# High DVE priority for the state updates, and the low-rank up-projections as two full products before two half-row ones

## Chip, cores and metric

The kernel runs on one core of a Trainium2 chip. The metric is the device time of one execution in microseconds. Engines are named as in the profile: PE is TensorE's matmuls, PEld its weight loads, DVE is VectorE, ACT ScalarE, POOL GpSimd, SP the queue that issues most transfers.

## What is computed

Two layers over 1024 tokens of width 1024. Each layer normalises its input, projects it, runs four mixers with 8 heads of 64, gates every mixer's output, and projects back:

```python
for l in range(DEPTH):                       # 2
    h = rms_norm(x, norm_pre[l])
    p = h @ w_in[l]
    (a_qk, a_v, a_o, a_z, a_i, a_f, b_sh, b_z, c_x, c_z, d_q, d_k, d_v, d_z) = split_at(...)
    h_a = mlstm_chunkwise(...)               # A: C = sc * C + (w v) k, out = C q
    b_sh = b_sh + rwkv_mu[l] * (token_shift(b_sh) - b_sh)
    r_b, k_b, v_b, w_lo, a_lo = split_at(b_sh, [G, G, G, LORA_W, LORA_A])
    decay_logit = rwkv_w0[l] + jnp.tanh(w_lo) @ rwkv_w_up[l]
    w_b = jnp.exp(-W_DECAY_SCALE * jax.nn.sigmoid(decay_logit))
    a_b = jax.nn.sigmoid(rwkv_a0[l] + a_lo @ rwkv_a_up[l])
    wkv = rwkv7_scan(...)                    # B: S = S (diag(w) - kh (a kh)) + v k, y = S r
    y_c = rglru(causal_dwconv(c_x, ...), ...) * silu(c_z)    # C
    o_d = retention_chunkwise(q_d, k_d, heads(d_v))          # D: R = g * R + k v
    y = jnp.concatenate([y_a, y_b, y_c, y_d], -1) @ w_out[l]
    x = x + rms_norm(y, norm_post[l])
```

`jnp.tanh(w_lo) @ rwkv_w_up` and `a_lo @ rwkv_a_up` are the two low-rank up-projections (64 inner columns each).

## The kernel before

**Units.** Every mixer works on four units of 128 channels (two heads): A0 to A3, B0 to B3, C0 to C3, D0 to D3. A unit has projection pieces (`ch_piece_of`, `tok_piece_of`: 24 matmuls of 512 columns for half of the tokens, or the like of 256, into the PSUM ring `pj`) and a mix; those of A, B and D go through the tokens in quarters of 256. In a layer a first stretch loads and normalises, a long middle runs projections and mixes together, and `out_product` multiplies the stored outputs by the output weights.

**Precision.** A float32 operand is split into two parts, `hi` and `lo`, of a faster type (`fp32r`), and a product is made of three matmuls. For the up-projections, `lu[0]` (tile `luh`) holds the high part of the weights twice, over 128 rows, and meets the token operand `lo_` (tile `lora`), whose 128 rows are high and low part; `lu[1]` (tile `lul`) is the low part of the weights, which meets the high part alone, so it takes 64 rows: the upper half for the decay (n = 0, result `wps`), the lower half for the other (n = 1, result `aps`). `prep` does this once for each quarter of each B unit, 4 x 4 x 2 = 32 times, and writes the head sums with `onesr` behind it.

**Unit B.** `prep` builds decays and scores; `invert` does a triangular inversion of 32 x 32 blocks on DVE, step by step (tiles `NT`, `inv`, `PA`); `mix` joins the blocks, makes `TQ` = [Q'|T] with four DVE subtractions from PSUM, and then walks four chunks of 64: a matmul of `TQ` with the state `bS`, and two DVE instructions (one for each head) that write the next `bS`, scaled by `wc`.

**Units A and D.** Per quarter: scores on PE and their weighting on DVE (`D`, a tile of the ring `t`), then two chunks of 128, each with a matmul that reads the state (`aS`, `dS`) and two DVE instructions that update it. The outputs are normalised (`ln_groups`, with a power on POOL) and, with a delay (`drv.later`), transposed on PE (`psmx<-ident,t` for A and D, `psbc<-ident,bl` for B) and stored.

**Order.** `Driver` writes the instructions in the order of a planner: the class `Clock` estimates when each engine is free, and a thread's next step is written when its `clock.step` plus a slack has passed and two PSUM banks of its ring are expected free; otherwise a projection step is written. For PE the planner adds `DRAIN` = 0.095 us when the kind of matmul changes, which is its rows, type and operation: `mode = (rows, w.dtype == F32R, name)`. The framework then lays out each engine's queue ahead of time, by its own timing: among the instructions that it expects to be ready, the one written first. `tc.high_priority()` makes the instructions written inside it count as written much earlier. On the chip each queue runs in the order so laid out. All records carry one helper's line (L255), so instructions are told apart by tiles.

Of the kernel before, what the change touches and what calls it, by code (L numbers as in the profile page):

```python
# [20 lines left out]
ALU = mybir.AluOpType  # L21
# [89 lines left out]
G128 = [float(np.exp(_log_g().astype(np.float64)[h] * 128.0)) for h in range(NH)]  # L111
# [25 lines left out]
QA = 256  # L137
QB = 256
# [123 lines left out]
def trunk(ctx: ExitStack, tc, x, wch, wa, wd, wg, wo, pv, gb, lup, lrw, npost, cst, dtab, out):  # L262
    nc = tc.nc
    clock = Clock()
    V, A, Pl, PE, DQ = (Timed(e, n, clock) for e, n in ((nc.vector, "DVE"), (nc.scalar, "ACT"), (nc.gpsimd, "POOL"), (nc.tensor, "PE"),
                                                        (nc.sync, "SP")))
# [83 lines left out]
    bS = [const.tile([128, 128], F32, tag=f"bS{i}", name=f"bS{i}") for i in range(2)]  # L350
# [422 lines left out]
    def unit_b(l, P, hTs, j, drv):  # L773
        rkvd = DT(f"rkv{l}_{j}", (3, 128, S))
        st = {"p": 0, "ready": -1, "inverted": -1}
# [32 lines left out]
        def prep(qt):  # L808
# [5 lines left out]
            lu = st["lu"]  # L814
# [6 lines left out]
            lo_ = T("lora", (128, 2, QB), F32R)  # L821
# [7 lines left out]
            wps = PT("bc")  # L829
            aps = PT("bc")  # L830
            for n, p in enumerate((wps, aps)):
                hp = slice(64 * n, 64 * n + 64)
                PE.matmul(p[:, 0:QB], lu[0][:, n, :], lo_[:, n, :], start=True, stop=False)
                PE.matmul(p[:, 0:QB], lu[1][hp], lo_[hp, n, :], start=False, stop=True)
            nps = PT("bc")
            head_sums(nps, kparts)
# [106 lines left out]
        def mix(qt):  # L943
# [62 lines left out]
            for p in range(CP):  # L1006
                for h, e in ((0, 0), (1, 1), (1, 0), (0, 1)):
                    PE.matmul(pss[e][64 * h:64 * h + 64, p * 128:(p + 1) * 128], AP[nrow(e), h * CP + p, :], Gt[nrow(e), h, 2 * p + e, 64:192], start=True, stop=True)
            for e in range(2):
                p3 = pss[e][:, 0:CP * 128].rearrange("p (c t) -> p c t", c=CP)  # L1010
                V.tensor_tensor(TQ[:, e::2, 0:64], AR[:, :, 2 + e, :], p3[:, :, 0:64], ALU.subtract)
                V.tensor_tensor(TQ[:, e::2, 64:128], id64.unsqueeze(1).to_broadcast((128, CP, 64)), p3[:, :, 64:128], ALU.subtract)
# [8 lines left out]
            for c in range(CB):  # L1021
                yc = yd[:, c * 128:(c + 1) * 128]
                n = qt * CB + c
                if n:
                    PE.matmul(yc, TQ[:, c, :], bS[n % 2], start=False, stop=True, skip_group_check=True)
                for h in range(2):
                    hp = slice(64 * h, 64 * h + 64)
                    V.tensor_scalar(bS[(n + 1) % 2][hp, hp], yc[64:128, hp], wc[64:128, h, c:c + 1], None, ALU.mult)
                if c + 1 < CB:
                    yield STEP  # L1030
            drv.flush("B")
# [57 lines left out]
    def unit_a(l, P, hTs, j, drv):  # L1089
# [28 lines left out]
        def mix():  # L1118
            yield lambda: st_["p"] == 8 and P.gates_done
            st = None  # L1120
            NQ = QA // 128
            for qt in range(S // QA):
                half, qo = divmod(qt * QA, H)
                q, k = qk[0, half][:, qo:qo + QA], qk[1, half][:, qo:qo + QA]
                c0 = qo // 128
                vq, oq = va[half][:, c0:c0 + NQ, :], tho[half][:, c0:c0 + NQ, :]
                gt = P.gT[:, 4 * half + c0:4 * half + c0 + NQ, :]
                ts_ = slice(qt * QA, (qt + 1) * QA)
                qsb = tq()
                for h in range(2):  # L1130
                    DQ.dma_start(qsb[64 * h:64 * h + 64, :], P.qdram[2 * j + h:2 * j + h + 1, ts_].to_broadcast((64, QA)))
                pk = []
                Ds = []
                for h in range(2):
                    D = tq()
                    DQ.dma_start(D, P.adram[2 * j + h:2 * j + h + 1, ts_].to_broadcast((128, QA)))
                    Ds.append(D)
                kt = tq()
                ps = PT("mx")
                for c in range(NQ):  # L1140
                    sl = slice(c * 128, c * 128 + 128)
                    PE.transpose(ps[:, sl], k[:, sl], ident)
                V.tensor_tensor(kt.rearrange("p (c h d) -> p c h d", c=NQ, h=2), ps[:, 0:QA].rearrange("p (c h d) -> p c h d", c=NQ, h=2),
                                gt[:, :, 8 + 2 * j:10 + 2 * j].unsqueeze(3).to_broadcast((128, NQ, 2, 64)), ALU.mult)
                for h in range(2):
                    D = Ds[h]
                    for c in range(NQ):
                        sl = slice(c * 128, c * 128 + 128)
                        V.scalar_tensor_tensor(D[:, sl], D[:, sl], gt[:, c, 2 * j + h:2 * j + h + 1], cap, ALU.add, ALU.min)
                    A.activation(D, D, AF.Exp)  # L1150
                yield STEP
                pss = [PT("mx"), PT("mx")]
                for c in range(NQ):
                    sl = slice(c * 128, c * 128 + 128)
                    for h in range(2):
                        hp = slice(64 * h, 64 * h + 64)
                        PE.matmul(pss[h][:, sl], k[hp, sl], q[hp, sl], start=True, stop=True)
                for h in range(2):
                    D = Ds[h]
                    V.scalar_tensor_tensor(D, pss[h][:, 0:QA], 1.0 / 32, D, ALU.mult, ALU.mult)  # L1160
                    pk.append(D)
                sc = small(NQ)
                V.tensor_copy(sc, qsb.rearrange("p (c t) -> p c t", t=128)[:, :, 127])
                q1 = qsb
                V.tensor_tensor(q1, q, qsb, ALU.mult)
                yield STEP
                xa = tq()
                dn = small(2 * NQ)
                for c in range(NQ):
                    sl = slice(c * 128, c * 128 + 128)  # L1170
                    o = PT("mx")
                    if st is not None:
                        PE.matmul(o[:, 0:130], q1[:, sl], st, start=True, stop=True)
                    for h in range(2):
                        PE.matmul(o[:, 65 * h:65 * h + 65], pk[h][:, sl], vq[:, c, 65 * h:65 * h + 65], start=(st is None and h == 0), stop=True, skip_group_check=True)
                    PE.matmul(o[:, 256:386], kt[:, sl], vq[:, c, :], start=True, stop=True)
                    o3 = o[:, 0:130].rearrange("p (h e) -> p h e", h=2)
                    V.scalar_tensor_tensor(xa[:, sl].rearrange("p (h e) -> p h e", h=2), oq[:, c, :].rearrange("p (h e) -> p h e", h=2),
                                           1.0, o3[:, :, 0:64], ALU.add, ALU.mult)
                    A.activation(dn[:, 2 * c:2 * c + 2], o3[:, :, 64], AF.Square)  # L1180
                    st2 = aS[(NQ * qt + c) % 2]
                    for h in range(2):
                        hp = slice(64 * h, 64 * h + 64)
                        if st is None:
                            V.tensor_copy(st2[hp, 65 * h:65 * h + 65], o[hp, 256 + 65 * h:256 + 65 * h + 65])
                            continue
                        V.scalar_tensor_tensor(st2[hp, 65 * h:65 * h + 65], st[hp, 65 * h:65 * h + 65], sc[hp, c:c + 1],
                                               o[hp, 256 + 65 * h:256 + 65 * h + 65], ALU.mult, ALU.add)
                    st = st2
                    yield STEP  # L1190

                V.tensor_tensor(dn.rearrange("p (c h) -> p c h", h=2), dn.rearrange("p (c h) -> p c h", h=2),
                                gt[:, :, 16 + 2 * j:18 + 2 * j], ALU.max)
                V.tensor_scalar(dn, dn, 4e-5, None, ALU.mult)
                drv.flush("A")
                yn = ln_groups(xa.rearrange("p (g d) -> p g d", d=64), 2 * NQ, dn, tq)
                if qt % 2 == 1:
                    drv.free += 4
                drv.later("A", lambda yn=yn, qt=qt: out_a(l, j, P.h_mnw, yn, qt))
                yield  # L1200
# [11 lines left out]
    def unit_d(l, P, hTs, j, drv):  # L1212
# [28 lines left out]
        def mix():  # L1241
# [3 lines left out]
            st = None  # L1245
            NQ = 2
            for qt in range(4):
# [29 lines left out]
                for c in range(2):  # L1277
# [9 lines left out]
                    for h in range(2):  # L1287
                        hp = slice(64 * h, 64 * h + 64)
                        if st is None:
                            V.tensor_copy(st2[hp, hp], o[hp, so + 64 * h:so + 64 * h + 64])  # L1290
                            continue
                        V.scalar_tensor_tensor(st2[hp, hp], st[hp, hp], G128[2 * j + h], o[hp, so + 64 * h:so + 64 * h + 64], ALU.mult, ALU.add)
                    st = st2
                    yield STEP
                ep = small(4)
# [282 lines left out]
```

## Time and profile before

| what | value |
|---|---|
| median of 3 runs | 2529.39 us (2527.3 to 2534.37) |
| profiled execution | 2524.98 us |
| its span, first to last instruction | 2523.1 us |
| PE busy | 2383.7 us, 94% |
| DVE busy | 1794.0 us, 71% |
| ACT busy | 1054.0 us, 42% |
| mean granted clock of PE | 0.992 |

The times of the rows below are microseconds from the start of the span unless marked ns. Busy time of a group is the union of its instructions; matmuls are pipelined, so one that is recorded as 0.38 us long may be followed by the next after 0.13 us. What PE spends on a matmul is read from the starts of neighbours in the timeline. The figure behind the bar of a group is the engine's idle time just before its instructions, and the arrows name what ended it.

### The profile page before, as it was taken

What the parts mean: (1) busy time and instruction counts of PE and PEld (TensorE: products, weight loads), DVE (VectorE), ACT (ScalarE), POOL (GpSimd) and SP (SyncE); (2) the same over time, 40 slices, a digit from 0 to 9 for tenths busy, and PEclk for the clock granted to TensorE, in tenths of its full rate; (3) what the DMA queues carried; (4) which work ended last, traced back from release to release, by engine and by line L of the source; (5) the groups of instructions that cost most, each with busy time, mean ns of one, the idle gap of its engine ahead of it and who ended that gap; (6) DMA issues with size and microseconds to landing.
All of it is one profiled execution on the core that took longest, in us unless ns stands there. A gap on an engine that the chain in (4) does not pass through costs nothing.

```text
span 2523.1 us, 45012 instructions
## 1 busy us (share of the span) xinstructions
PE 2383.7 (94%) x16032; PEld 1955.2 (77%) x16032; DVE 1794.0 (71%) x5724; ACT 1054.0 (42%) x2325; POOL 193.7 (8%) x306
## 2 busy tenths in 40 slices
PE   7999999999999999999999999999999999999998
PEld 5797887787787777887677878877877877788876
DVE  6678878878778875435577787888788778744464
ACT  5334433543543553323354344335445435522233
POOL 1201100010000000000012001000000000000000
PEclk9999999999999999999999999999999999999999
DMA  5323233232222233655633232332323222326564
GB/s 160 101 72 88 62 78 99 67 84 71 91 76 75 75 88 103 194 162 176 196 119 103 68 93 74 78 90 68 81 72 90 69 79 76 102 94 217 172 198 153
DMA packets 219237, 265.82 MB, mean 105 GB/s; under 512 B 72708, under 2 KB 122244, under 8 KB 219012
## 3 DMA queue, kind: packets, MB, share of 16 engines
q1 hardware_dynamic: 210308, 254.54, 33.9%
q0 software_dynamic: 8704, 8.39, 1.4%
q8 instruction: 127, 2.08, 0.3%
q14 instruction: 98, 0.80, 0.1%
HBM read 201.76 MB, written 61.08 MB: 104 GB/s over the span
## 4 chain that ended last, share of the span: by engine, by line
PE 47%; DVE 28%; DMA 10%; issue 8%; POOL 4%; ACT 2%; SPq 2%; DVEq 0%; POOLq 0%; ACTq 0%
PE pspj L255 31%; PE psbc L255 9%; PE psmx L255 7%; DVE NT L255 4%; DVE pr L255 4%; DMA PA<-pd 4%; DVE t L255 3%; DVE lo L255 2%; DVE bS L255 2%; POOL sm L255 2%; DVE bt L255 2%; DMA raw<-in_wo_dram 2%; DVE inv L255 2%; SPq L255 2%; DVE sm L255 1%
## 5 line engine op out<-in xcount | busy, mean ns | idle before, releaser
L255 PE MATMUL pspj<-hT,hi 128*128 128x512 f32 x2880 | 940.2, 405 | 2.1 <-DVE hT L255 1.4
L255 PEld LDWEIGHTS pspj<-hT,hi 128*128 128x128 f32 x2880 | 522.0, 190 | 106.7 <-issue 2.5
L255 PE MATMUL pspj<-hT,lo 128*128 128x512 f32 x1440 | 569.8, 396 | 0.0
L255 ACT CAST hi<-raw 128x512 fp32r<-128x512 f32 x372 | 230.0, 619 | 470.0 <-PE pspj L255 266.2
L255 PE MATMUL pspj<-hi,hT 128*128 128x256 f32 x2048 | 409.9, 290 | 0.0
L255 DVE TENSOR_TENSOR lo<-raw,hi 128x512 fp32r<-128x512 f32 x372 | 257.2, 693 | 152.4 <-ACT hi L255 150.9
L255 PEld LDWEIGHTS pspj<-hi,hT 128*128 128x128 f32 x2048 | 331.5, 192 | 6.7 <-issue 1.6
L255 PEld LDWEIGHTS pspj<-hT,lo 128*128 128x128 f32 x1440 | 272.5, 189 | 58.9 <-DVE lo L255 0.2
L255 PE MATMUL pspj<-lo,hT 128*128 128x256 f32 x1024 | 291.1, 284 | 0.1
L255 PEld LDWEIGHTS pspj<-lo,hT 128*128 128x128 f32 x1024 | 197.0, 192 | 0.8 <-DVE lo L255 0.5
L255 POOL TENSOR_TENSOR sm<-sm,mhalf 128x4 f32<-128x4 f32 (+1 forms) x96 | 90.8, 946 | 1227.1 <-DVE sm L255 1141.4
L255 DVE SCALAR_TENSOR_TENSOR NT<-PA,NT 128x23 f32<-128x23 f32 (+13 forms) x768 | 142.9, 235 | 49.0 <-DMA PA<-pd 45.4
L255 PE MATMUL psbc<-hi,pr 128*128 128x512 f32 x384 | 130.7, 394 | 0.0
L255 PE MATMUL pspj<-hi,pr 128*128 128x512 f32 x384 | 130.7, 394 | 0.0
L255 DVE SCALAR_TENSOR_TENSOR pr<-c,pv,pr 128x512 f32<-128x512 f32 x144 | 107.3, 745 | 15.8 <-ACT pr L255 14.9
L255 ACT ACTIVATE t<-t 128x256 f32<-128x256 f32 (+1 forms) x132 | 53.9, 411 | 150.7 <-DVE t L255 126.7
L255 PE MATMUL psmx<-pr,t 128*128 128x65 f32 (+3 forms) x768 | 108.3, 276 | 0.2 <-DVE t L255 0.2
L255 PEld LDWEIGHTS psmx<-pr,t 128*128 128x128 f32 x768 | 96.9, 192 | 1.3 <-DVE t L255 0.3
L255 PE MATMUL psmx<-hi,pr 128*128 128x512 f32 x256 | 91.2, 397 | 3.5 <-ACT pr L255 2.0
L255 DVE TENSOR_TENSOR inv<-PA,NT 128x24 f32<-128x24 f32 (+13 forms) x480 | 87.1, 181 | 8.4
L255 DVE TENSOR_TENSOR NT<-NT,inv 128x24 f32<-128x24 f32 (+13 forms) x480 | 86.6, 180 | 7.2
L255 DVE TENSOR_SCALAR bS<-psbc,wc 64x64 f32<-64x64 f32 x256 | 74.2, 290 | 17.2 <-PE psbc L255 9.8
(273 smaller groups left out, 3824.2 us busy)
## 6 DMA issues: line engine op xcount, KB each, us to landing
raw<-in_wch_dram SPq DMA_DIRECT2D x180, 256.0 KB
raw<-in_wo_dram SPq DMA_DIRECT2D x128, 256.0 KB
PA<-pd SPq DMA_DIRECT2D x64, 256.0 KB
zmix<-c SPq DMA_DIRECT2D x64, 256.0 KB
rkv<-ymix SPq DMA_DIRECT2D x64, 256.0 KB
rkv<-c SPq DMA_DIRECT2D x48, 256.0 KB
rkv<-rkv SPq DMA_DIRECT2D x32, 384.0 KB
lora<-lora POOLq DMA_DIRECT2D x32, 256.0 KB, 3.5
```

Of the source, the lines that this page charges most:

```text
L255: res = fn(*args, **kw)
```

## The change

In `prep` of unit B the four matmuls of the up-projections are written in another order: first the two 128-row products (n = 0, 1), then the two 64-row ones. Five kinds of DVE instruction are put inside `tc.high_priority()`: the four subtractions into `TQ`, the two updates of `bS`, the weighting of unit A's scores, and the updates of `aS` and `dS`. Operands, results and instruction counts stay as they are.

```diff
             for n, p in enumerate((wps, aps)):
+                PE.matmul(p[:, 0:QB], lu[0][:, n, :], lo_[:, n, :], start=True, stop=False)
+            for n, p in enumerate((wps, aps)):
                 hp = slice(64 * n, 64 * n + 64)
-                PE.matmul(p[:, 0:QB], lu[0][:, n, :], lo_[:, n, :], start=True, stop=False)
                 PE.matmul(p[:, 0:QB], lu[1][hp], lo_[hp, n, :], start=False, stop=True)
...
-            for e in range(2):
+            with tc.high_priority():
+              for e in range(2):
                 p3 = pss[e][:, 0:CP * 128].rearrange("p (c t) -> p c t", c=CP)
                 V.tensor_tensor(TQ[:, e::2, 0:64], AR[:, :, 2 + e, :], p3[:, :, 0:64], ALU.subtract)
                 V.tensor_tensor(TQ[:, e::2, 64:128], id64.unsqueeze(1).to_broadcast((128, CP, 64)), p3[:, :, 64:128], ALU.subtract)
...
-                for h in range(2):
-                    hp = slice(64 * h, 64 * h + 64)
-                    V.tensor_scalar(bS[(n + 1) % 2][hp, hp], yc[64:128, hp], wc[64:128, h, c:c + 1], None, ALU.mult)
+                with tc.high_priority():
+                    for h in range(2):
+                        hp = slice(64 * h, 64 * h + 64)
+                        V.tensor_scalar(bS[(n + 1) % 2][hp, hp], yc[64:128, hp], wc[64:128, h, c:c + 1], None, ALU.mult)
...
-                    V.scalar_tensor_tensor(D, pss[h][:, 0:QA], 1.0 / 32, D, ALU.mult, ALU.mult)
+                    with tc.high_priority():
+                        V.scalar_tensor_tensor(D, pss[h][:, 0:QA], 1.0 / 32, D, ALU.mult, ALU.mult)
...
-                        V.scalar_tensor_tensor(st2[hp, 65 * h:65 * h + 65], st[hp, 65 * h:65 * h + 65], sc[hp, c:c + 1],
-                                               o[hp, 256 + 65 * h:256 + 65 * h + 65], ALU.mult, ALU.add)
+                        with tc.high_priority():
+                            V.scalar_tensor_tensor(st2[hp, 65 * h:65 * h + 65], st[hp, 65 * h:65 * h + 65], sc[hp, c:c + 1],
+                                                   o[hp, 256 + 65 * h:256 + 65 * h + 65], ALU.mult, ALU.add)
...
-                        V.scalar_tensor_tensor(st2[hp, hp], st[hp, hp], G128[2 * j + h], o[hp, so + 64 * h:so + 64 * h + 64], ALU.mult, ALU.add)
+                        with tc.high_priority():
+                            V.scalar_tensor_tensor(st2[hp, hp], st[hp, hp], G128[2 * j + h], o[hp, so + 64 * h:so + 64 * h + 64], ALU.mult, ALU.add)
```

## Rows read from the trace of the kernel before

**Rows 1.** The page's first part: busy us of each engine, its share, instructions
```profile
PE 2383.7 (94%) x16032; PEld 1955.2 (77%) x16032; DVE 1794.0 (71%) x5724; ACT 1054.0 (42%) x2325; POOL 193.7 (8%) x306
```

**Rows 2.** The page's fourth part: the chain that ended last, by engine
```profile
PE 47%; DVE 28%; DMA 10%; issue 8%; POOL 4%; ACT 2%; SPq 2%; DVEq 0%; POOLq 0%; ACTq 0%
```

**Rows 3.** Table by stretch: from:to, length, busy us of each engine, clock, DMA
```profile
60.00:960.00 900.00, 849.76 (x6423) 706.44 (x6422) 710.94 (x2481) 398.33 (x912) 82.11 (x124) 0.99 0.30 82
1310.00:2210.00 900.00, 848.64 (x6437) 703.98 (x6436) 712.91 (x2481) 399.15 (x913) 82.15 (x124) 0.99 0.29 82
...
1300.00:1400.00 100.00, 96.81 (x530) 82.27 (x530) 69.68 (x180) 39.59 (x81) 14.77 (x15) 0.98 0.32 97
2100.00:2200.00 100.00, 90.75 (x618) 70.30 (x617) 78.50 (x268) 53.99 (x111) 8.35 (x11) 1.00 0.29 84
```

**Rows 4.** Timeline of PE at one place: start, length, operation, out<-in
```profile
184.81 0.36 PE L255 MATMUL psbc<-lora,luh 128*128 128x256 f32 x1
185.10 0.38 PE L255 MATMUL psbc<-lora,lul 64*128 64x256 f32 x1
185.41 0.39 PE L255 MATMUL psbc<-lora,luh 128*128 128x256 f32 x1
185.72 0.38 PE L255 MATMUL psbc<-lora,lul 64*128 64x256 f32 x1
186.03 0.38 PE L255 MATMUL pspj<-hi,hT 128*128 128x256 f32 x1
186.25 0.28 PE L255 MATMUL pspj<-lo,hT 128*128 128x256 f32 x1
186.38 0.28 PE L255 MATMUL pspj<-hi,hT 128*128 128x256 f32 x1
```

**Rows 5.** Groups of PE: busy us, mean ns | idle before; one timeline row
```profile
L255 PE MATMUL psbc<-lora,lul 64*128 64x256 f32 x64 | 24.4, 382 | 0.0
L255 PE MATMUL psbc<-lora,luh 128*128 128x256 f32 x64 | 23.1, 360 | 0.0
...
439.00 0.71 PE L255 MATMUL psmx<-t,t 64*128 64x128 f32 x8
```

**Rows 6.** Groups of PE that read a state or an output, with releasers
```profile
L255 PE MATMUL psbc<-bS,TQ 128*128 128x128 f32 x240 | 53.8, 306 | 19.9 <-DVE bS L255 14.5 <-DVE TQ L255 3.9
L255 PE MATMUL psmx<-ident,t 128*128 128x128 f32 x128 | 27.0, 293 | 20.7 <-DVE t L255 17.2 <-DVE NT L255 3.5
L255 PE MATMUL psmx<-aS,t 128*128 128x130 f32 x112 | 24.8, 303 | 8.4 <-DVE aS L255 5.3 <-PE psbc L255 1.7 <-issue 0.9
L255 PE MATMUL psmx<-dS,t 128*128 128x128 f32 x112 | 24.3, 299 | 7.1 <-DVE dS L255 7.1
L255 PE MATMUL psbc<-ident,bl 128*128 128x128 f32 x64 | 13.2, 288 | 19.9 <-DVE bl L255 15.2 <-DVE NT L255 3.8 <-DVE sm L255 0.9
```

**Rows 7.** Waits of weight loads and matmuls: us, times, longest us
```profile
PEld psbc L255 <- DVE bS L255: 35.0, 61, 1.7
...
PE psbc L255 <- DVE bS L255: 14.5, 27, 1.5
```

**Rows 8.** Timeline of DVE, then PE, around one wait for bS
```profile
439.21 0.42 DVE L255 TENSOR_TENSOR t<-t,sm 128x256 f32<-128x256 f32 x1 [0.90 <-POOL sm L255]
440.05 0.21 DVE L255 TENSOR_TENSOR NT<-NT,inv 128x45 f32<-128x45 f32 x1
440.29 0.29 DVE L255 TENSOR_SCALAR bS<-psbc,wc 64x64 f32<-64x64 f32 x1
440.61 0.20 DVE L255 TENSOR_TENSOR inv<-PA,NT 128x42 f32<-128x42 f32 x1
440.85 0.29 DVE L255 TENSOR_SCALAR bS<-psbc,wc 64x64 f32<-64x64 f32 x1
...
441.19 0.49 PE L255 MATMUL psbc<-bS,TQ 128*128 128x128 f32 x2 [1.48 <-DVE bS L255]
```

**Rows 9.** The group of the bS updates on DVE
```profile
L255 DVE TENSOR_SCALAR bS<-psbc,wc 64x64 f32<-64x64 f32 x256 | 74.2, 290 | 17.2 <-PE psbc L255 9.8
```

## The prediction

> **What bounds the kernel now.** I read the busy shares first: TensorE (PE) is busy in 94% of the span, VectorE (DVE) in 71% [rows 1]. The chain that ended last runs through PE for 47% and through DVE for 28% [rows 2]; it hops between the two, so it does not say which of them sets the pace, and I went on to the table by stretch. In the long middle of each layer, where all four head groups are mixed while projections run, PE is busy 849.76 and 848.64 of 900 us and DVE 710.94 and 712.91 [rows 3]. So PE works almost without a break, and the two layers repeat each other within 1.2 us. A microsecond of PE work taken out is worth nearly a microsecond; DVE matters only where PE stands idle for it, and of that there is some 50 us in each middle (900 - 849.76 = 50.2, 900 - 848.64 = 51.4).
>
> **Part 1: the low-rank up-projections.** In the PE timeline of one such place [rows 4] the four matmuls start at 184.81, 185.10, 185.41 and 185.72, and the first matmul of something else at 186.03. They take 186.03 - 184.81 = 1.22 us of PE, 0.29 to 0.31 each. Ordinary matmuls of the same 256 columns start 0.13 apart (186.25 to 186.38). The difference, some 0.18, lies at each change between the full array (128*128) and half its rows (64*128); the first ordinary matmul behind a change also holds the next one up to 0.22 instead of 0.13 (186.03 to 186.25). The lines group shows 64 + 64 such matmuls and no idle time before them [rows 5], so there are 32 places and 32 x 1.22 = 39 us. The old order full, half, full, half makes four changes per place (one into each half, one out of each); full, full, half, half makes two.
>
> After the change, start to start: full to full 0.13, from the row of ordinary neighbours, or 0.22 if the first one's entry still holds up the second; full to half 0.31, as now; half to half unknown, since the trace has no two half-row matmuls of this type behind one another; half to the next 0.31, as now. For the unknown one the nearest row is the half-row score products of unit D: eight in 0.71 us, so 0.71 / 8 = 0.09 apart at most [rows 5]. They use the upper and lower rows in turn, as the two new ones do. I take 0.06, between 0 (both start together) and 0.13 (one after the other). That gives 0.13 + 0.31 + 0.06 + 0.31 = 0.81, a saving of 0.41 per place and 13.1 us in all. Bounds: 0.75 at best (saving 0.47, 15.0 us), 0.22 + 0.31 + 0.13 + 0.31 = 0.97 (0.25, 8.0 us), and if half to half also costs a full change, 1.15 (0.07, 2.2 us). I see no loss: the same four matmuls with no change added.
>
> What PE saves reaches the end except where PE only gets sooner to a stall: I count it at PE's busy share of the middle, 849.76 / 900 = 0.944, so 12.4 us. The decay result is complete about 0.15 later (0.13 + 0.31 against 0.29 before its last matmul), the other about 0.4 sooner; ScalarE reads both and is 44% busy there (398.33 of 900 us [rows 3]), and DVE behind it has other work. Costed at nothing; uncovered it would be 32 x 0.15 = 5 us.
>
> The Trainium skill (TensorEngine Tiling, Key Properties) says that changing the tiling mode, not just the tile, drains TensorE; it gives no price. TensorE: Matmul & The Clock Gate (Single matmul latency) puts the part of a lone matmul that a stream hides at about 166 ns; two fewer of these in 32 places would be an estimate of 10.6 us where the rows above give 13.1. The same page (Measured speedup vs the span model) lets matmuls on different rows start about 4 ns apart; by that the sum is at its upper end, 15 us. No row here shows that for this type.
>
> **Part 2: high priority on DVE.** It adds and removes no instruction. It moves 256 updates of bS at 0.290 us [rows 9], 128 subtractions into TQ, 64 score products and the updates of aS and dS ahead of other ready work in DVE's queue. It can gain only where PE waits for one of them. Summing what PE waited for in its own groups [rows 6]: bS 14.5, TQ 3.9, aS 5.3, dS 7.1, together 30.8 us. One such stall is in full view [rows 8]: before its bS pair DVE runs an unrelated normalisation (which itself waits 0.90 us for POOL) and steps of the triangular inversion; one more such step stands between the two halves of the pair (440.29, then 440.85); PE starts at 441.19 after 1.48 us idle. With priority the two halves stand together and ahead of what was ready with them.
>
> Bounds: 30.8 us if every one of these stalls goes. Nothing if PE's queue moves along: its order too is laid out by when operands are expected, and the trace shows that the matmul already stands right behind its update, since 61 of 240 weight loads wait for bS, 35.0 us, and 27 matmuls, 14.5 us [rows 7]. An update that is expected earlier then gets its matmul earlier, and the next lateness of DVE makes PE wait again. Below nothing too: what is overtaken is late next (rival D). I take a quarter, 8 us: the step between the two halves of a pair really goes, and in rows 8 it is 440.85 - 440.29 - 0.29 = 0.27 of the 1.48 us, 18%; of the wait behind the queue and POOL I count a little on top.
>
> **Part 3: the planner.** The order of writing comes from a planner with its own clock, which counts 0.095 us for each change of matmul kind. Two fewer per place shift its clock by 0.19 us each time, 6 us in all, so steps of other units come due at other places from the first up-projection on. DVE priority it does not see. This is a redraw of the stalls without a sign. Its size: over the 18 stretches of 100 us in the two middles PE's busy time runs from 90.75 to 96.81 us [rows 3], standard deviation 1.6; 18 independent draws would spread by 1.6 x the root of 18 = 7 us. I count 0 and keep 7 us either way.
>
> **Sum.** The profiled execution took 2524.98 us, its span 2523.1 and 1.9 around it; it lies 4.4 under the median of the three times, 2529.39. On its own time: 2524.98 - 12.4 - 8 = 2504.6. Against the median: 2529.4 - 20.4 = 2509.
>
> **Rivals.** A, the up-projections alone: the PE queue moves along and no stall shrinks. For it: the waits of rows 7. Against: the foreign step inside the pair in rows 8. 2529.4 - 12.4 = 2517.
>
> B, everything comes off: all 30.8 us of stalls go as well, 2529.4 - 12.4 - 30.8 = 2486. Against: DVE is busy 79% in the middle, and something is always late next.
>
> C, the redraw of part 3 goes against it by about two of its spreads, 16 us: 2525. For: the planner's clock shifts at 32 places. Against: the two layers, which have nearly the same order, show nearly the same stalls, so nothing makes another order worse as such.
>
> D, slower: priority pushes back the DVE work of the output normalisations, which PE transposes wait for. Those waits are already the largest in the middle: 20.7 us before the transposes of t and 19.9 before those of bl [rows 6], in 64 + 32 places (two transposes each). If a place waits behind one more bS pair, that is 0.58 us; for all, 96 x 0.58 = 56 us; at the share of time that DVE is busy, 0.79, it is 44, and the time 2529.4 - 20.4 + 44 = 2553. It decides from 28 us on (20.4 to lose and 7.6 beyond), an average of 0.29 us per place, half a pair. Against: a pair is short and the outputs are written with a delay.
>
> E, the change does not do what it says: the second full product waits for its PSUM bank and the old order returns on PE. Then only part 2 stands, 2529.4 - 8 = 2521. Against: the planner asks for two free banks before it begins.
>
> **How the numbers follow.** Forecast 0.43, A 0.20, B 0.08, C 0.13, D 0.11, E 0.05. What a measurement of this kernel can tell from no change is about 0.3%, 7.6 us. Faster than 2521.8: 0.40 of the forecast, 0.14 of A, B 0.08, 0.02 of C, 0.03 of E, together 0.67. Slower than 2537: D, 0.11. Within: 0.22. The range leaves out most of D at the top and the far part of B at the bottom: 2484 (all of B's gain) to 2533 (C with half a spread more).
>
> **What would show it.** Up-projections: in the PE timeline luh, luh, lul, lul, the next matmul 0.75 to 0.97 us behind the first instead of 1.22; 1.15 would show that half to half changes too. Priority: the two halves of a bS pair next to each other with no inversion step between, and PE's idle time before bS, aS and dS matmuls at some 27 instead of 35.4 us (the three groups of rows 6 together); unchanged means A, near zero B. D shows as idle time above 60 us before the transposes of t and bl (40.6 now). The redraw shows as other stretches being the poor ones and the two middles no longer at 50 us of idle time. The prediction is wrong if the stalls do not add up to what the rows name, above all if PE's idle time in the middles grows by more than the 13 us of work that leaves.

## The result and the profile after

| | before | after |
|---|---|---|
| median of four runs each | 2528.35 us (2523.91 to 2534.37) | 2497.8 us (2495.79 to 2500.21) |
| ratio of the runs, 95% interval | | 0.9879 [0.9859, 0.9898] |
| profiled execution, its span | 2524.98, 2523.1 us | 2497.11, 2495.4 us |

The change takes 30.6 us off (1.2%). 20.4 were forecast, and the time lies within the range of 2484 to 2533. The experiments below show that the sum came out near for other reasons than those it was made of.

The first part of the page after, the engines' busy time and share. It answers [rows 1]:

```profile
PE 2354.5 (94%) x16032; PEld 1945.6 (78%) x16032; DVE 1793.1 (72%) x5724; ACT 1049.1 (42%) x2325; POOL 196.5 (8%) x306
```

PE's busy time fell by 29.2 us with the same 16032 matmuls, about as much as the whole time did; its idle time is as large as before (139.4 of 2523.1 us then, 140.9 of 2495.4 now). The long middles as a table by stretch (length, then busy us of PE, PEld, DVE, ACT, POOL, clock, DMA), for [rows 3]:

```profile
60.00:960.00 900.00, 847.46 (x6448) 711.09 (x6446) 709.90 (x2466) 398.15 (x917) 83.14 (x124) 0.99 0.29 83
1300.00:2200.00 900.00, 849.66 (x6504) 712.75 (x6503) 715.53 (x2486) 399.97 (x919) 83.20 (x124) 0.99 0.30 84
```

Busy shares are as before; more matmuls are done in the same 900 us (6448 for 6423, 6504 for 6437). The place of [rows 4] in the timeline of PE after:

```profile
182.17 0.48 PE L255 MATMUL psbc<-lora,luh 128*128 128x256 f32 x2
182.58 0.38 PE L255 MATMUL psbc<-lora,lul 64*128 64x256 f32 x2
182.89 0.38 PE L255 MATMUL pspj<-hi,hT 128*128 128x256 f32 x1
183.12 0.28 PE L255 MATMUL pspj<-lo,hT 128*128 128x256 f32 x1
```

Two full, two half, and the next matmul 182.89 - 182.17 = 0.72 us behind the first, where it was 1.22: the order on PE is the one written, and 0.50 us of PE work is gone at this place; in 32 such places that is 16 us. The two halves lie in one record of 0.38 us, as long as one of them alone in [rows 4]: they run together. PE and PEld groups that read a state or an output (busy us, mean ns | idle us before, releasers), for [rows 6]:

```profile
L255 PE MATMUL psbc<-bS,TQ 128*128 128x128 f32 x240 | 50.1, 290 | 16.5 <-DVE bS L255 10.8 <-DVE TQ L255 5.0
L255 PEld LDWEIGHTS psbc<-bS,TQ 128*128 128x128 f32 x240 | 40.2, 189 | 32.4 <-DVE bS L255 20.8 <-DVE TQ L255 7.0
L255 PE MATMUL psmx<-aS,t 128*128 128x130 f32 x112 | 24.1, 297 | 11.8 <-DVE aS L255 5.4 <-issue 4.7 <-PE psbc L255 1.7
L255 PE MATMUL psmx<-dS,t 128*128 128x128 f32 x112 | 24.2, 298 | 3.9 <-DVE dS L255 3.6 <-DVE hl L255 0.3
L255 PE MATMUL psmx<-ident,t 128*128 128x128 f32 x128 | 26.6, 290 | 23.0 <-DVE t L255 17.6 <-DVE NT L255 4.1 <-ACT cc L255 1.2
L255 PE MATMUL psbc<-ident,bl 128*128 128x128 f32 x64 | 13.2, 288 | 13.8 <-DVE bl L255 5.0 <-DVE NT L255 4.6 <-ACT c L255 1.9
```

By PE's idle times the priority would have done next to nothing: 16.5 + 11.8 + 3.9 = 32.2 us ahead of the three state matmuls, where the kernel before had 35.4. That is the first sign that the idle time in PE's own rows doesn't account for the 30 us.

### The profile page after: what moved, and what is told of

Same layout as the page of the kernel before. It is cut to its first block, busy times and chain, and to the rows that moved or that the text cites. A ratio compares the mean times of both kernels' runs of the same rounds, so it can differ in the third digit from the quotient of the medians.

```text
span 2495.4 us, 44964 instructions
## 1 busy us (share of the span) xinstructions
PE 2354.5 (94%) x16032; PEld 1945.6 (78%) x16032; DVE 1793.1 (72%) x5724; ACT 1049.1 (42%) x2325; POOL 196.5 (8%) x306
## 4 chain that ended last, share of the span: by engine, by line
PE 21%; DVE 15%; DMA 7%; issue 5%; POOL 2%; ACT 1%; SPq 1%; DVEq 0%; POOLq 0%; ACTq 0%
PE pspj L255 14%; PE psbc L255 4%; PE psmx L255 3%; DVE NT L255 2%; DVE pr L255 2%; DMA raw<-in_wo_dram 2%; DMA PA<-pd 2%; DVE lo L255 1%; DVE t L255 1%; POOL sm L255 1%; DMA rkv<-ymix 1%; DVE bS L255 1%; DVE sm L255 1%; SPq L255 1%; DVE bt L255 1%
## 5 line engine op out<-in xcount | busy, mean ns | idle before, releaser
L255 DVE SCALAR_TENSOR_TENSOR NT<-PA,NT 128x23 f32<-128x23 f32 (+15 forms) x768 | 143.1, 238 | 44.7 <-DMA PA<-pd 41.5
```

What stands on the lines that cost most here:

```text
L255: res = fn(*args, **kw)
```

## Experiments

Each kernel is compared with runs of the kernel before on the same chip, taken beside it; their medians are 2517 to 2520 us. A ratio of 0.990 is 25 us.

### The new order of the up-projections, with and without the planner

Three runs take the first part of the change apart. The order on the chip and what the planner's clock is told are two things, since the planner can be told separately (`nc.tensor` writes a matmul behind its back). In `e1_order` both are new, in `e3_order_noplan` only the chip's order, in `e4_plan_only` only the planner's. Three ideas of where the 30 us come from stand against each other in the expectations. Theory 1: PE's saved work reaches the end, nearly all of its 16 us. Rival 1: the other order of writing, drawn by a planner that counts differently (the redraw), carries a large part. Rival 2: the time that PE saves runs into later stalls.

```diff
 e3_order_noplan (e4_plan_only is the reverse: old order in nc.tensor, new order in clock.op)
             for n, p in enumerate((wps, aps)):
+                nc.tensor.matmul(p[:, 0:QB], lu[0][:, n, :], lo_[:, n, :], start=True, stop=False)
+            for n, p in enumerate((wps, aps)):
                 hp = slice(64 * n, 64 * n + 64)
-                PE.matmul(p[:, 0:QB], lu[0][:, n, :], lo_[:, n, :], start=True, stop=False)
-                PE.matmul(p[:, 0:QB], lu[1][hp], lo_[hp, n, :], start=False, stop=True)
+                nc.tensor.matmul(p[:, 0:QB], lu[1][hp], lo_[hp, n, :], start=False, stop=True)
+            for n, p in enumerate((wps, aps)):
+                clock.op("PE", "matmul", (p[:, 0:QB], lu[0][:, n, :], lo_[:, n, :]), {})
+                clock.op("PE", "matmul", (p[:, 0:QB], lu[1][64 * n:64 * n + 64], lo_[64 * n:64 * n + 64, n, :]), {})
```

> The up-projections in the new order on the chip, but the planner's clock is told the old order, so that everything else is written as before; no priority. Theory 1: 15 us less than before (16 us of PE work x 0.944), 2513, the same as with the planner told. Rival 2 (saved PE time runs into later stalls): 5 us less, 2523. If this differs from the run in which the planner sees the new order by more than 4 us, the difference is the redraw.

> The reverse: the up-projections in the old order on the chip, the planner's clock told the new order; no priority. What is left is the redraw of the order of writing alone. Theory 1: within 7 us of before either way, 2521 to 2535, since a redraw has no sign. Rival 1 (the redraw carries a large part): 10 us less or more, under 2518.

> Only the up-projections in the new order, no priority; the planner sees the new order too. Theory 1 (the time goes by PE work saved: in the trace after, such a place takes 0.725 us where it took 1.23, so 0.5 x 32 = 16 us, of which 0.944 reach the end): 15 us less than before, 2513 us, and the other half of the 30 us is the priority's. Rival 1 (the redraw of the planner's order carries a large part of the 30 us): 25 us less or more, 2503. Rival 2 (the saved PE time runs into later stalls): 5 us less, 2523.

Measured: order alone 1.0011 [0.9998, 1.0024], plan alone 0.9915 [0.9894, 0.9936], both 0.993 [0.9913, 0.9947].

So the new order on PE gains nothing that shows (`e3_order_noplan` is 3 us slower, within its error; with the new plan, `e1_order` is 4 us slower than `e4_plan_only`, their intervals overlapping). The order of writing that the planner draws when it is told of it is worth 21 us, although on the chip the old matmuls run. Theory 1 falls on both counts. Where the 16 us go is seen where the two traces are laid beside each other, since in `e3_order_noplan` nearly every matmul keeps its position: 15896 of 16032 stand at the same place in PE's queue. One place in the timeline of PE of the kernel before:

```profile
448.20 0.36 PE L255 MATMUL psbc<-lora,luh 128*128 128x256 f32 x1
...
449.44 0.49 PE L255 MATMUL pspj<-hT,hi 128*128 128x512 f32 x1
450.17 0.49 PE L255 MATMUL psmx<-dS,t 128*128 128x128 f32 x2 [0.24 <-DVE dS L255]
```

And in that of `e3_order_noplan`:

```profile
443.56 0.48 PE L832 MATMUL psbc<-lora,luh 128*128 128x256 f32 x2
443.97 0.38 PE L835 MATMUL psbc<-lora,lul 64*128 64x256 f32 x2
444.28 0.50 PE L255 MATMUL pspj<-hT,hi 128*128 128x512 f32 x1
445.52 0.49 PE L255 MATMUL psmx<-dS,t 128*128 128x128 f32 x2 [0.74 <-DVE dS L255]
```

The place takes 0.72 instead of 1.24 us, and the wait for `dS` right behind it takes 0.74 instead of 0.24: from the first up-projection to the matmul with `dS` it is 1.97 us before and 1.96 now. Over all 32 places together, the time from the first up-projection to the next other matmul is 38.5 us before and 22.3 here. Matching the matmuls of the two traces in order, I followed the lead that each place gives up to the next wait of PE over 0.1 us, which in half of the places comes within some 20 matmuls: in 19 it is gone to within 0.02 us, in 3 more than gone, in 6 there is 0.13 to 0.42 us left; in 2 PE did not wait soon, and in 2 a fall of the clock hides it. The page of `e3_order_noplan`:

```profile
span 2522.3 us, 45010 instructions
...
PE 2375.4 (94%) x16032; PEld 1952.9 (77%) x16032; DVE 1794.8 (71%) x5724; ACT 1050.6 (42%) x2325; POOL 193.7 (8%) x306
```

PE's busy time is 8.3 us lower, its idle time 7.5 higher (2522.3 - 2375.4 = 146.9 for 139.4). That the busy time fell by 8 and not by 16 fits the clock that PE was granted: as a mean over these two traces 0.989 of full speed for 0.992, and over all runs 0.9886 in 12 of `e3_order_noplan` and 0.9914 in 16 of the kernel before. A lower share means PE work that takes longer.

### Is a redraw of the planner good by itself?

Two more runs leave the instructions as in the kernel before and only move the planner's clock at the 32 places, which can change the order in which they are written.

```diff
 e8_plan_plus / e9_plan_minus_half, behind the four matmuls
+            clock.free["PE"] += 0.19        # e9: -= 0.095
```

> The kernel before with the planner's clock moved the other way: 0.19 us added at each of the 32 places instead of taken off; what runs on the chip is unchanged apart from the order of writing. If the 21 us of the run with the new plan alone have a direction (a planner that counts less for the up-projections orders better): the same or slower than before, ratio 1.000 to 1.010. If a redraw has no direction: either way, ratio anywhere in 0.990 to 1.010, and a second fast one would say that the order of before was a poor draw.

> A third redraw: the kernel before with 0.095 us taken off the planner's clock at each of the 32 places (half of what the change takes off), nothing else. If redraws spread without direction around a mean below the order of before: ratio between 0.990 and 1.002. If the gain grows with the amount taken off: about 0.996, half of the 0.9915 of the full amount.

Measured: `e8_plan_plus` 0.9959 [0.9946, 0.9971], `e9_plan_minus_half` 0.9997 [0.9986, 1.0008].

0.19 us less per place gave -21 us, 0.19 more -10 us, 0.095 less nothing. But the third is no redraw: in the trace of `e9_plan_minus_half`, 16024 of the 16032 matmuls stand at the same place in PE's queue as in the kernel before, and 5718 of 5724 instructions in DVE's. In `e4_plan_only` it is 10602 matmuls, in `e8_plan_plus` 5554. So the planner's choices hardly changed, and the run shows only that nearly the same program takes the same time. That leaves three orders, that of before among them, at 0, -0.41 and -0.85%. The gain doesn't follow the sign of the shift; whether before was an unlucky draw can't be told from two others. The page of `e4_plan_only`:

```profile
span 2491.6 us, 44927 instructions
...
PE 2364.0 (95%) x16032; PEld 1949.2 (78%) x16032; DVE 1796.4 (72%) x5724; ACT 1051.7 (42%) x2325; POOL 197.2 (8%) x306
```

What in the new order of writing saves the time I could not pin to a wait: the waits that PE shows fell by 12 us (139.4 to 2491.6 - 2364.0 = 127.6), spread over many groups, its busy time by 20. That stays open.

### The priority, and its parts

```diff
 e2_prio: the five high-priority blocks of the change, nothing else
 e7_prio_b: of these the two of unit B (TQ, bS)
 e11_prio_ad: of these the three of A and D (scores, aS, dS)
```

All three keep the old order and the planner's order of before, since the planner does not see the priority. What the framework lays out for PE moves a little with it: in `e7_prio_b` 15244 of the 16032 matmuls stand at their old place in the queue, in `e11_prio_ad` 15342.

> Only the five kinds of high priority, the up-projections in the old order, so that the planner writes exactly the order of before. Theory 1: the rest of the 30 us, 15 us less than before, 2513, with the two halves of every bS pair next to each other. Rival A of the prediction (the PE queue moves along): within 3 us of before, 2528. Rival B (all 30.8 us of stalls go): 2498.

> Only unit B's priority (the updates of bS and the subtractions into TQ), old order of the up-projections, old plan. All five kinds together gave 0.993 of before. If the gain comes from the bS pairs that stand together (256 of the 544 updates, and PE's idle time before their matmul fell from 19.9 to 9.9 us there): 0.7 or more of it, ratio 0.995 or lower. If it comes from aS, dS and the scores: ratio 0.998 or higher.

> Only the priority of aS, dS and the scores, old order, old plan. If it costs as the difference of the two earlier runs says: 1.0034, with more idle time of PE before the transposes of t and of bl. If those updates help by themselves as the idle time before their matmuls (8.4 and 7.1 us) suggests and only crowd unit B's: 0.997 or lower.

Measured: all five 0.993 [0.9914, 0.9947], unit B's 0.9896 [0.9879, 0.9912], A's and D's 1.0 [0.999, 1.001].

Unit B's priority alone is worth 26 us, more than all five together. That it is not merely another order of PE's queue is made likely by `e11_prio_ad`, which moves nearly as many matmuls and gains nothing. TQ and bS were not run apart. In the timeline of DVE of `e7_prio_b` the two halves of a pair are one record, with nothing between them as there was in [rows 8]:

```profile
433.71 0.20 DVE L255 TENSOR_TENSOR NT<-NT,inv 128x45 f32<-128x45 f32 x1
433.95 0.59 DVE L255 TENSOR_SCALAR bS<-psbc,wc 64x64 f32<-64x64 f32 x2
434.57 0.20 DVE L255 TENSOR_TENSOR inv<-PA,NT 128x42 f32<-128x42 f32 x1
```

Over the whole trace, 32 of the 128 pairs stood together in the kernel before and all 128 do here; from the start of the first half to the end of the second a pair takes 1.05 us on average before and 0.60 here. The groups of the matmul that reads bS, first in the kernel before (its PE row is in [rows 6]), then in `e7_prio_b`:

```profile
L255 PEld LDWEIGHTS psbc<-bS,TQ 128*128 128x128 f32 x240 | 38.4, 190 | 43.5 <-DVE bS L255 35.0 <-DVE TQ L255 6.0
```

```profile
L255 PE MATMUL psbc<-bS,TQ 128*128 128x128 f32 x240 | 49.8, 289 | 8.8 <-DVE bS L255 6.1 <-DVE TQ L255 2.5
L255 PEld LDWEIGHTS psbc<-bS,TQ 128*128 128x128 f32 x240 | 40.7, 191 | 21.8 <-DVE bS L255 14.4 <-DVE TQ L255 2.8
```

PE's idle time fell by 19.9 - 8.8 = 11.1 us, that of the weight loads by 43.5 - 21.8 = 21.7. The second is near the 26 us measured, the first is not even half: a matmul's recorded length reaches past the point where the next could have started (0.28 us recorded where neighbours start 0.13 apart [rows 4]), so a wait of a tenth or two of a microsecond is no idle time of PE in the rows. The starts say the same: from the start of the matmul before to that of a matmul with bS it is 71.8 us in all in the kernel before and 51.8 here, 20 us less. The two traces lie 2523.1 - 2487.9 = 35.2 us apart, more than the 26 us of the runs; what is left is spread over other groups. The page of `e7_prio_b`:

```profile
span 2487.9 us, 45010 instructions
...
PE 2360.2 (95%) x16032; PEld 1949.6 (78%) x16032; DVE 1786.7 (72%) x5724; ACT 1050.1 (42%) x2325; POOL 192.9 (8%) x306
```

PE's busy time is 23.5 us lower with the very same matmuls, so the busy time of before held waits; a part may be the clock, 0.994 of full speed in this trace for 0.992.

`e11_prio_ad` shows rival D of the prediction at work, in small:

```profile
L255 PE MATMUL psbc<-ident,bl 128*128 128x128 f32 x64 | 14.0, 302 | 32.6 <-DVE bl L255 21.7 <-DVE NT L255 5.5 <-DVE inv L255 5.4
L255 PE MATMUL psmx<-aS,t 128*128 128x130 f32 x112 | 24.3, 298 | 4.9 <-DVE aS L255 2.8 <-issue 1.5 <-PE psbc L255 0.5
L255 PE MATMUL psmx<-dS,t 128*128 128x128 f32 x112 | 24.1, 297 | 3.5 <-DVE dS L255 3.5
```

Before aS and dS PE waits 8.4 us now instead of 15.5, before the transposes of bl 32.6 instead of 19.9 [rows 6]: 7.1 won, 12.7 lost; the transposes of t wait 5 us less, and the time is that of before.

### How much is PE's work worth, and DVE's?

```diff
 e5_pe_twice: the four matmuls written twice, the first time behind the planner's back
 e6_dve_more, in prep:
             V.tensor_tensor(AR[:, :, 2:4, :], c4(r), Wp[:, :, :, 1:65], ALU.mult)
+            for _ in range(3):
+                nc.vector.tensor_tensor(AR[:, :, 2:4, :], c4(r), Wp[:, :, :, 1:65], ALU.mult)
```

> The kernel before with the four up-projection matmuls of each place run twice (the result is the same; the planner is told of one set), so 4 more matmuls and 4 more changes of shape in 32 places: 1.22 x 32 = 39 us more PE work and nothing else. Theory P (the prediction's: PE sets the pace, a microsecond of its work is worth 0.94): 37 us slower than before. Theory W (PE is paced by waits that come again every few microseconds, so what one place saves or costs is taken up by the next wait, as the run with the new order and the old plan suggests, where 16 us of saved PE work changed nothing): clearly less, 10 to 25 us slower, with PE's idle time lower by what is missing.

> The kernel before with one DVE product of each preparation (128x256, 0.417 us) run three more times (same result, planner not told): 1.25 x 32 = 40 us more DVE work. Theory P (PE sets the pace; DVE has a fifth of its time free in the middle): under 12 us slower. Theory W (what PE waits for is the DVE queue, so its work goes nearly straight into the time): 25 to 40 us slower.

Measured: `e5_pe_twice` 1.0055 [1.0037, 1.0074], `e6_dve_more` 1.0 [0.9987, 1.0012].

Some 39 us more PE work cost 14 us, a little over a third. The rest came out of PE's waits. The page of `e5_pe_twice`, and its group of the transposes of t:

```profile
span 2529.1 us, 45270 instructions
...
PE 2411.1 (95%) x16160; PEld 1977.9 (78%) x16160; DVE 1797.7 (71%) x5724; ACT 1055.8 (42%) x2325; POOL 191.9 (8%) x306
...
L255 PE MATMUL psmx<-ident,t 128*128 128x128 f32 x128 | 26.5, 289 | 12.2 <-DVE t L255 11.0 <-DVE NT L255 1.1
```

Idle are 2529.1 - 2411.1 = 118.0 us, 21 less than in the kernel before, the largest part of it before the transposes of t (20.7 to 12.2). So theory P falls and theory W holds for PE. But its other half falls as well: three more products in each place cost nothing (within 3 us). The page of `e6_dve_more`, and the group of the added products:

```profile
PE 2380.3 (95%) x16032; PEld 1954.9 (78%) x16032; DVE 1820.8 (72%) x5820; ACT 1054.2 (42%) x2325; POOL 191.2 (8%) x306
...
L870 DVE TENSOR_TENSOR AR<-rkv,bt 128x256 f32<-128x256 f32 x96 | 40.6, 423 | 0.1
```

They take 40.6 us by their own row; DVE's busy time rose by 26.8 (1794.0 to 1820.8), since neighbouring records overlap. DVE is not the pace either, at this place; there it had time to spare. My reading is that what counts is whether the result that PE waits for next comes later, and neither share of busy time tells that.

Neither price is clean: beside the added work, the framework laid out the rest a little differently (704 of the other 15904 matmuls of `e5_pe_twice` and 640 of `e6_dve_more` stand at another place in PE's queue). So the 14 us and the 0 can hold a small redraw. That the 39 us of work cost far less than the 37 us of theory P is clear; the exact share isn't.

### The parts together

```diff
 e12_order_b_noplan: e7_prio_b and the new order of e3_order_noplan, planner told the old one
 e10_order_plan_b: the change without the priority of the scores, aS and dS
```

> Unit B's priority with the new order of the up-projections, planner told the old order. Priority alone gave 0.9896, the new order alone 1.0011. If the saved 16 us of PE work count as soon as PE waits less for bS: 0.985 or lower. If they still run into the next wait: 0.988 to 0.991.

> The change without the priority of aS, dS and the scores: new order of the up-projections, new plan, priority for bS and TQ alone. In the old plan unit B's priority alone gave 0.9896 and all five kinds 0.993, so the other three cost 0.34%. If they cost the same here: 0.9845, faster than the change (0.9879) and than every other version. If the parts do not add up, since they remove the same waits: 0.988 to 0.991.

Measured: `e12_order_b_noplan` 0.9895 [0.9881, 0.991], `e10_order_plan_b` 0.9859 [0.9843, 0.9875].

The new order adds nothing to unit B's priority either (0.9895 beside 0.9896). `e10_order_plan_b` is the fastest kernel of the study; its interval overlaps that of the change (0.9879 [0.9859, 0.9898]), so that it beats it is likely and not shown. One way through the versions, with 1% as 25 us:

| step | ratio | us |
|---|---|---|
| before, then unit B's priority | 0.9896 | -26 |
| and the new order on PE | 0.9895 | 0 |
| and the planner told | 0.9859 | -9 |
| and the priority of scores, aS, dS: the change | 0.9879 | +5, not clear of 0 |

Taken on its own the redraw gave 21 us, here 9. The parts may take away some of the same waits, or the planner's new order is just another draw for another program; the runs don't decide that. The way through matters: with the new plan the time from the matmul ahead to the matmul with bS is 60.5 us in `e10_order_plan_b` and 61.6 in the change, so only 10 of the 20 us that `e7_prio_b` saved there are left.

## Why the prediction was right, and where its steps were wrong

**Part 1, the work.** The reading of the timeline was right and the price on the low side: 0.50 us per place where 0.41 was taken, just over the upper bound of 0.47. Two full ones stand 0.12 apart, or 0.20 behind a float32 matmul; from full to half it is 0.21 and not 0.31, as the first two matmuls of the old order already had it behind a projection (0.29 in [rows 4] is behind a float32 matmul); 0.31 is what a full one behind a half costs, and a half behind such a full one. Half to half is 0.003 us. The trace of before held that too: the "0.09 apart at most" was an average over eight score products, which start in pairs some 7 ns apart, with 0.1 to 0.2 us between the pairs. The sentence on the Trainium skill (TensorE: Matmul & The Clock Gate, Measured speedup vs the span model), some 4 ns between matmuls on different rows, was the better guide: the runs agree with it for this type too, with 3 ns. The sum from the nearest rows was 3 us short of the 16.

**Part 1, its worth.** This is the step that failed. "A microsecond of PE work taken out is worth nearly a microsecond", priced at PE's busy share of 0.944, gave 12.4 us; measured are +3, +4 and 0 us beside three different companions (old plan, new plan, unit B's priority), none clear of 0, the first with an error of 3 us. The busy share is an average over a stretch, and PE waits again soon behind 30 of the 32 places, 2 to 92 matmuls after the last up-projection. What the next wait behind the place is, had to be looked up: it stood in the trace (the 0.24 us for dS behind the place at 448.20).

**Part 2.** The mechanism was right (the step inside the pair goes), the size was not: 8 us taken, 18 measured for all five, 26 for unit B's, of a bound of 30.8. The quarter came from one stall, in which 0.27 us (18%) stood between the halves; over all 128 pairs the priority shortened a pair by 0.45 us. And the bound itself was read from PE's idle time alone, which hides short waits; the weight loads in [rows 7], quoted there for another purpose, had the 35.0 us. That aS, dS and the scores belong to the gain (12.4 of the 30.8) was wrong: their waits went to bl, as rival D has it; alone they gain nothing, and beside unit B's priority they cost 8 us in the old plan.

**Part 3.** "I count 0 and keep 7 us either way" was too narrow: 21 us from the plan of the change alone. The spread was worked out as of 18 independent stretches, but both layers are written in nearly the same order, so there are 9, each counted twice: 1.6 x 2 x the root of 9 = 9.6 us. The two shifts that did redraw the order (-21 and -10) fit that better, though -21 is more than twice of it.

**The rivals.** A (the up-projections alone, 2517) had the parts the wrong way round. B's time (2486) was too low. C, a redraw against it, came out as a redraw in its favour. D happened in small, before the transposes of bl. E did not happen. That 2509 and 2497.8 lie near is luck: 12 us that did not come were replaced by 18 to 26 of priority, where 8 were counted, and 9 or more of redraw. The range held for its width, not for its terms.

**What was to show it.** 0.72 us per place: seen, beyond the good end. The halves of the pairs together: seen. Idle time before the three state matmuls at 27: it is 32.2, although the time fell by more than forecast, because most of what was won never was idle time in these rows. Transposes above 60 us: 36.8. The two middles no longer at 50 us of idle time, as the sign of a redraw: they are at 52.5 and 50.3, and still the redraw came, so that sign was none.

## What to carry to other kernels

Before an engine's work is priced, look up the next wait of that engine behind the place: work saved ahead of a wait for another engine lengthens the wait, however busy the engine is, and a run with the piece doubled shows roughly what a microsecond more costs there, as far as the order of the rest stays. For waits on PE read the weight loads beside the matmuls, since short waits hide in the matmuls' recorded lengths. And where a planner's clock decides the order of the whole program, a change that touches its clock needs a run in which the planner is told the old story; otherwise a redraw of 10 to 20 us is taken for the effect. Whether a run that was to move the order did move it is seen in its trace, not in its edit.

## What the runs showed of the hardware

Two half-row matmuls of 256 columns on different rows start 3 to 4 ns apart in all 32 places of `e3_order_noplan` and take 0.38 us together, as much as one: the second is free, once nothing full stands between them.

With work taken off PE, its clock was lower. Granted is either the full 2.4 GHz or, for a few microseconds at a time, 1.2 GHz; the mean share over all runs is lower with the new order on PE in each of the three pairs (0.9886 for 0.9914, 0.9912 for 0.9932, and on two chips 0.9892 for 0.9925). `e9_plan_minus_half`, nearly the program of before, has 0.9922 for 0.9910, so a difference of 0.001 alone says nothing. One such fall in `e3_order_noplan`, as a table by stretch (length, busy us of PE, PEld, DVE, ACT, POOL, clock, DMA):

```profile
680.00:684.00 4.00, 4.00 (x23) 3.31 (x22) 3.81 (x20) 2.08 (x6) 0.00 (x0) 1.00 0.52 148
684.00:688.00 4.00, 1.31 (x8) 0.65 (x6) 3.16 (x9) 3.22 (x9) 0.99 (x1) 0.99 0.21 40
688.00:692.00 4.00, 3.44 (x11) 2.50 (x12) 3.02 (x7) 0.56 (x1) 1.55 (x3) 0.50 0.14 26
```

PE worked without a break, then 1.31 of 4 us, and then had half the clock. That the longer waits behind the saved work brought such falls about is likely and not shown for each. Over the runs of the kernel before, the time rises by about 1.3 us for each 0.001 of the share that is missing; by that, as an estimate, the 0.002 to 0.003 between the pairs are 3 to 4 us of the 16.
